# First weight block on ScalarE's queue in halves, input rows 1 and 2 issued behind row 0, row 1 cast in halves

## The chip, the cores and the metric

The kernel runs on one core of one Trainium2 chip. The metric is the device time of one execution in microseconds (us), as the median of several runs. The engines are TensorE (PE in the profile; its weight loads are PEld), VectorE (DVE), ScalarE (ACT), GpSimd (POOL) and SyncE (SP). Loads are issued by the queues of SP, ACT or POOL and are carried by 16 DMA engines.

## The reference

One decoder block with two token mixers and a SwiGLU. The input is 512 tokens of width 1024 in float32; the depth is one layer.

```python
h = rms_norm(x, norm_mix_pre[l])
proj = h @ w_in[l]
(g_q, g_k, g_v, g_r, g_a, n_q, ..., n_gate, merge_gla, merge_nsa) = jnp.split(proj, split_points, axis=-1)
o_gla = gla_mixer(g_q, g_k, g_v, g_r, g_a, ...)      # chunked gated linear attention, 4 heads
o_nsa = nsa_mixer(n_q, ..., n_gate, ...)             # compressed + selected + window attention, 8 heads
mixed = (jax.nn.sigmoid(merge_gla) * (o_gla @ w_proj_gla[l])
         + jax.nn.sigmoid(merge_nsa) * (o_nsa @ w_proj_nsa[l]))
x = x + rms_norm(mixed @ w_out[l], norm_mix_post[l])
h = rms_norm(x, norm_ffn_pre[l])
f = (jax.nn.silu(h @ w_ffn_gate[l]) * (h @ w_ffn_up[l])) @ w_ffn_down[l]
x = x + rms_norm(f, norm_ffn_post[l])
```

The change concerns how the first input and weights reach the first projection `h @ w_in`.

## The kernel before

**Arithmetic.** Each large product is made of three: an operand is split into a high part (a copy cast to float32r, mostly on ScalarE) and a low part (the remainder, a subtraction on VectorE), and TensorE adds high x high, high x low and low x high.

**Input.** The host passes x transposed, `xT`, as 8 blocks of 128 features by 512 tokens. Here such a block is called row k of the input. Each is loaded into `X[:, k]` on SP's queue (line 258); ScalarE writes its high part `hT` with the norm's gain `g_pre` as a scale (line 261), VectorE the low part `hTl` (line 262). The gain is part of `vecs`, loaded on ScalarE's queue (line 145). The rms factor is applied later, to the products. Before the loop stand `warm`, a small Exp on ScalarE (line 143, with the table load that it brings), and eight products `spin` on TensorE (line 148).

**Weights.** `Stream` loads and splits the weights in an order planned ahead: `ahead_to` takes a raw tile `wraw` (three buffers), calls `fetch` to issue its load on SP's queue, and issues the cast (line 79) and the subtraction (line 85). The first block, `("tok", 0, 0)`, holds 880 columns: 440 for row 0 and 440 for row 1. It alone stands in `halved`: it is loaded in two halves (line 55), the first half is cast on VectorE and the second on ScalarE (line 73), and both are subtracted on VectorE (line 74). In the loop over k, `ahead_to` is called at k = 0 for the first block and at k = 2 for the second, so SP's issues come in this order:

```
row 0, first half of block 0, second half of block 0, row 1, row 2, block 1, row 3, ..., row 7, block 2
```

**First products.** `tok_chunk` (lines 314 to 316) makes the first token-wise projection: for each of 4 blocks of 128 tokens and each row k, three products of 440 columns, into four PSUM banks (`ps_mm`, `ps_sc`). Four such chunks use the 8 rows. After it comes the same with 368 columns (into `ps_tp`, `ps_acc`), and then the paired projections at line 412, whose weight forms are prepared by ScalarE and VectorE at lines 224, 348, 351, 382 and 383, with raw weights loaded at line 344.

**Order.** The Tile framework takes the instructions in the order of the text as priorities and, when the program is built, fixes an order on each engine by what is ready; `issue_after` and `high_priority` in the text put single instructions behind or ahead. All waits are derived from the data.

Of the kernel before, what the change touches and what calls it, by code (L numbers as in the profile page):

```python
# [8 lines left out]
F32 = mybir.dt.float32  # L9
F32R = mybir.dt.float32r  # L10
U8 = mybir.dt.uint8
AF = mybir.ActivationFunctionType
# [24 lines left out]
class Stream:  # L37
# [7 lines left out]
    def plan(self, key, ap, cols):  # L45
        self.src.append((key, ap if isinstance(ap, list) else [ap], cols))

    def fetch(self, raw, aps):
        at = 0
        for ap in aps:  # L50
            n = ap.shape[-1]
            if len(ap.shape) == 3:
                self.nc.sync.dma_start(raw.rearrange("p (k n) -> p k n", k=2)[:, :, at:at + n], ap)
            else:
                self.nc.sync.dma_start(raw[:, at:at + n], ap)
            at += n

    def ahead_to(self, n):
        while self.made < min(n, len(self.src)):
            i = self.made  # L60
            key, aps, cols = self.src[i]
            raw = self.pool.tile([128, 1024], F32, tag="wraw", bufs=3, name="wraw")
            cut = self.halved.get(key, cols)
            parts = [slice(0, cut)] + ([slice(cut, cols)] if cut < cols else [])
            self.fetch(raw[:, :cols], [aps[0][:, p] for p in parts] if cut < cols else aps)
            if key in self.place:
                hi, lo = self.place[key]()
            else:
                hi = self.pool.tile([128, 1024], F32R, tag="whi", bufs=2, name="whi")
                lo = self.pool.tile([128, 1024], F32R, tag="wlo", bufs=2, name="wlo")  # L70
            if cut < cols:
                for p, copy in zip(parts, (self.nc.vector.tensor_copy, self.nc.scalar.copy)):
                    copy(hi[:, p], raw[:, p])
                    self.nc.vector.tensor_tensor(out=lo[:, p], in0=raw[:, p], in1=hi[:, p].bitcast(F32),
                                                 op=OP.subtract)
                self.done[i] = (hi, lo)
                self.made += 1
                continue
            self.cast = self.nc.scalar.copy(hi[:, :cols], raw[:, :cols])  # L79
            if key in self.on_dma:  # L80

                self.nc.scalar.activation(out=lo[:, :cols], in_=raw[:, :cols], func=AF.Copy, scale=-1.0)  # L82
                self.nc.gpsimd.dma_start(lo[:, :cols], raw[:, :cols], accum_op=OP.add)  # L83
            else:
                self.nc.vector.tensor_tensor(out=lo[:, :cols], in0=raw[:, :cols], in1=hi[:, :cols].bitcast(F32),  # L85
                                             op=OP.subtract)
            self.done[i] = (hi, lo)
            self.made += 1
# [24 lines left out]
def hybrid_block_kernel(ctx: ExitStack, tc: tile.TileContext, I, outT):  # L113
    nc = tc.nc
    act, dve, pool, pe = nc.scalar, nc.vector, nc.gpsimd, nc.tensor

    base = ctx.enter_context(tc.tile_pool(name="base", bufs=1, reuse_waits="tile"))
# [12 lines left out]
    mhalf = base.tile([128, 16], F32, name="mhalf")  # L130
# [8 lines left out]
        pool.dma_start(t, I[name])  # L139
        return t  # L140

    warm = base.tile([128, 1], F32, name="warm")
    act.activation(out=warm, in_=mhalf[:, 0:1], func=AF.Exp)
    vecs = base.tile([128, 4 * KD + HG + 2], F32, name="vecs")
    act.dma_start(vecs, I["vecs"])
    spin = bank("acc")
# [2 lines left out]
    g_pre, g_post = vecs[:, 0:8], vecs[:, 8:16]  # L149
    g_fpre, g_fpost = vecs[:, 16:24], vecs[:, 24:32]  # L150
    b_alpha, g_gla = vecs[:, 32:36], vecs[:, 36:38]
    hT = base.tile([128, KD, S], F32R, name="hT_hi")
# [27 lines left out]
    for key in with_gla + with_cmp + with_att + late:  # L180
        kind, n = key
# [74 lines left out]
    X = xin.tile([128, KD, S], F32, name="xt")  # L256
    for k in range(KD):
        nc.sync.dma_start(X[:, k], I["xT"][k])
        if k % 2 == 0:
            tk.ahead_to(min(k // 2 + 1, 2))  # L260
        last = act.activation(out=hT[:, k, :], in_=X[:, k], func=AF.Copy, scale=g_pre[:, k:k + 1])
        dve.scalar_tensor_tensor(out=hTl[:, k, :], in0=X[:, k], scalar=g_pre[:, k:k + 1],
                                 in1=hT[:, k, :].bitcast(F32), op0=OP.mult, op1=OP.subtract)
    p_mid = tc.tile_pool(name="mid", bufs=1, reuse_waits="tile")
# [1354 lines left out]
    for n in range(N0, KF):  # L1619
# [3 lines left out]
        last = unit(n, rest_of_forms if n == N0 else None)  # L1623
# [317 lines left out]
```

## Time and profile before

| | before |
|---|---|
| runs | 847.33 us median of 3 (847.05 to 847.94) |
| the profiled execution | 847.33 us |
| its span | 845.5 us |
| TensorE busy | 833.6 us (99%) |
| VectorE, ScalarE busy | 646.2 us (76%), 532.2 us (63%) |
| TensorE clock granted | 0.999 |
| loaded and stored | 119.96 MB, mean 142 GB/s |

The span goes from the first to the last instruction that the profile has; the rest of the execution's time lies around it. Times in the trace count from the span's start. In the order-of-time view a row has start, length, engine, line, operation and tiles; a bracket gives the engine's idle time ahead of it and what ended it. Rows of "SPq" or "ACTq" are issues of loads by those queues. In the view by stretches, a row gives for each engine the busy time and the number of instructions, then the granted clock, the mean busy share of the 16 DMA engines and GB/s.

### The profile page before, as it was taken

To read this page: it belongs to the slowest core of one execution; us is meant where nothing else is said; L and a number is where in the kernel's file an instruction comes from. 1 tells how busy PE (TensorE), PEld (TensorE's weight loads), DVE (VectorE), ACT (ScalarE), POOL (GpSimd) and SP (SyncE) were. 2 spreads that over 40 slices of the span, in tenths; PEclk is the share of its full clock that TensorE was granted. 3 is DMA by queue.
4 is the path that set the end of the run, shared out by engine and by line. 5 is a ranking of instruction groups with operands and counts; after the bars stand their busy time and mean duration, and the time that the engine had idled before them with its cause. 6 is when DMAs were issued, how large, how long until landed. Compare 5 with 4: busy or idle time off the path is not lost.

```text
span 845.5 us, 14860 instructions
## 1 busy us (share of the span) xinstructions
PE 833.6 (99%) x5640; PEld 763.4 (90%) x5640; DVE 646.2 (76%) x1209; ACT 532.2 (63%) x961; POOL 159.4 (19%) x194
## 2 busy tenths in 40 slices
PE   9999999999999999999999999999999999999997
PEld 8999999877888788788888998999999999889996
DVE  7877989845657888887685398998777779739885
ACT  7766686455635989887545587666555667435442
POOL 0223222322300010001001363021211110001433
PEclk9999999999999999999999999999999999999999
DMA  7688787211432445444238769488877762325222
GB/s 249 146 211 190 173 175 155 76 50 53 124 109 74 101 107 119 105 120 97 54 113 293 226 150 243 116 214 204 188 198 185 184 156 63 109 79 174 89 100 100
DMA packets 45017, 119.96 MB, mean 142 GB/s; under 512 B 5933, under 2 KB 11325, under 8 KB 44817
## 3 DMA queue, kind: packets, MB, share of 16 engines
q1 hardware_dynamic: 30576, 82.49, 30.6%
q0 software_dynamic: 13648, 35.98, 23.5%
q8 instruction: 44, 0.72, 0.3%
q10 hardware_dynamic: 720, 0.54, 0.2%
q14 instruction: 29, 0.23, 0.1%
HBM read 104.31 MB, written 4.19 MB: 128 GB/s over the span
## 4 chain that ended last, share of the span: by engine, by line
PE 85%; ACT 6%; DVE 5%; issue 2%; DMA 1%; POOL 1%; SPq 0%; DVEq 0%; ACTq 0%; POOLq 0%
PE ps_mm L1481 6%; PE ps_mm L207 6%; PE ps_mm L209 6%; PE ps_mm L208 6%; PE ps_sc L1481 6%; PE ps_tp L1481 6%; PE ps_acc L1481 5%; PE ps_sc L1773 4%; PE ps_mm L412 3%; PE ps_tp L412 3%; PE ps_sc L412 2%; PE ps_acc L1773 2%; PE ps_mm L1773 2%; PE ps_acc L412 2%; PE ps_tp L1082 2%
## 5 line engine op out<-in xcount | busy, mean ns | idle before, releaser
L79 ACT CAST whi<-wraw 128x1024 fp32r<-128x1024 f32 (+3 forms) x58 | 56.3, 971 | 52.9 <-issue 18.5
L207 PE MATMUL ps_mm<-hT_hi,whi 128*128 128x512 f32 x168 | 68.5, 408 | 0.0
L209 PE MATMUL ps_mm<-hT_hi,wlo 128*128 128x512 f32 x168 | 66.2, 394 | 0.0
L208 PE MATMUL ps_mm<-hT_lo,whi 128*128 128x512 f32 x168 | 66.2, 394 | 0.0
L85 DVE TENSOR_TENSOR wlo<-wraw,whi 128x1024 fp32r<-128x1024 f32 (+3 forms) x43 | 47.0, 1093 | 21.3 <-ACT whi L79 21.2
L83 POOL DMA_DIRECT2D wlo<-wraw x15 | 12.9, 862 | 157.1 <-ACT wlo L82 157.1
L1042 ACT ACTIVATE p<-p,mx 128x512 f32<-128x512 f32 (+1 forms) x64 | 35.9, 560 | 8.8 <-DVE mx L1040 8.2
L225 DVE TENSOR_TENSOR pl<-ps_tp,ph 128x512 fp32r<-128x512 f32 (+1 forms) x64 | 31.0, 489 | 13.2 <-ACT ph L224 12.6
L209 PEld LDWEIGHTS ps_mm<-hT_hi,wlo 128*128 128x128 f32 x168 | 31.5, 188 | 7.1 <-DVE wlo L85 0.3
L207 PEld LDWEIGHTS ps_mm<-hT_hi,whi 128*128 128x128 f32 x168 | 31.6, 188 | 6.0
L208 PEld LDWEIGHTS ps_mm<-hT_lo,whi 128*128 128x128 f32 x168 | 31.7, 189 | 5.0
L1040 DVE CUSTOM_DVE_ANT_0 p<-ps_sc,causal 128x512 f32<-128x512 f32 (+1 forms) x64 | 30.2, 485 | 6.2 <-PE ps_sc L1033 5.9
L1380 POOL DMA_DIRECT2D w_uu<-in_w_up x19 | 16.4, 865 | 89.3 <-ACT w_uu L1378 20.4
L224 ACT CAST ph<-ps_tp 128x512 fp32r<-128x512 f32 (+1 forms) x64 | 26.4, 415 | 4.1 <-PE ps_tp L1082 3.5
L1082 PE MATMUL ps_tp<-ident,p 128*128 128x128 f32 x160 | 27.7, 273 | 0.4 <-ACT pc L976 0.2
L1082 PEld LDWEIGHTS ps_tp<-ident,p 128*128 128x128 f32 x160 | 20.6, 140 | 8.1 <-ACT pc L976 0.7
L1396 ACT CAST w_d1h<-s 128x1024 fp32r<-128x1024 f32 x13 | 13.6, 1049 | 20.6 <-issue 12.7
L207 PE MATMUL ps_mm<-gla_hi,whi 128*128 128x512 f32 x64 | 26.2, 409 | 0.0
L209 PE MATMUL ps_mm<-gla_hi,wlo 128*128 128x512 f32 x64 | 25.2, 394 | 0.0
L208 PE MATMUL ps_mm<-gla_lo,whi 128*128 128x512 f32 x64 | 25.2, 393 | 0.0
L1396 ACT CAST w_hl<-s 128x1024 fp32r<-128x1024 f32 x12 | 12.6, 1047 | 16.6 <-issue 14.7
L1396 ACT CAST w_d0h<-s 128x1024 fp32r<-128x1024 f32 x13 | 13.6, 1047 | 13.8 <-issue 12.7
(1234 smaller groups left out, 3363.9 us busy)
## 6 DMA issues: line engine op xcount, KB each, us to landing
wraw<-in_w_t SPq DMA_DIRECT2D x29, 512.0 KB, 3.7
wraw<-in_w_gate SPq DMA_DIRECT2D x21, 512.0 KB, 5.7
rw<-in_w_up SPq DMA_DIRECT2D x19, 512.0 KB, 4.2
wlo<-wraw POOLq DMA_DIRECT2D x15, 512.0 KB, 4.5
wlo<-in_w_gate POOLq DMA_DIRECT2D x13, 512.0 KB, 7.1
urw<-in_w_t SPq DMA_DIRECT2D x11, 512.0 KB, 5.6
w_uu<-in_w_up POOLq DMA_DIRECT2D x19, 256.0 KB, 5.7
wraw<-in_w_proj SPq DMA_DIRECT2D x8, 512.0 KB, 3.5
```

What stands on the lines that cost most here:

```text
L79: self.cast = self.nc.scalar.copy(hi[:, :cols], raw[:, :cols])
L85: self.nc.vector.tensor_tensor(out=lo[:, :cols], in0=raw[:, :cols], in1=hi[:, :cols].bitcast(F32), op=OP.subtract)
L207: pe.matmul(ps[:, t], wh[:, c], xh(k)[:, t], start=(k == 0), stop=False)
L208: pe.matmul(ps[:, t], wh[:, c], xl(k)[:, t], start=False, stop=False)
L209: marks.append(pe.matmul(ps[:, t], wl[:, c], xh(k)[:, t], start=False, stop=(k == ktot - 1)))
L225: dve.tensor_tensor(out=lo, in0=src, in1=hi.bitcast(F32), op=OP.subtract)
L412: pe.matmul(o, w[:, c], x_of(b, q, low), start=(first and q == 0 and i == 0), stop=(q == 3 and i == 2), skip_group_check=True)
L1042: act.activation(out=o, in_=o, func=AF.Exp, scale=-1.0, bias=mx[:, i:i + 1], accum_out=z[:, i:i + 1])
L1082: pe.transpose(tp[:, i * 128:(i + 1) * 128], p[:, OFF[i] + k * 128:OFF[i] + (k + 1) * 128], ident)
L1396: act.copy(hi, t)
L1481: pe.matmul(o, w[:, c], x[q], start=(first and q == 0 and i == 0), stop=(q == 3 and i == 2), skip_group_check=True)
L1773: pe.matmul(o, w[:, c], x[q], start=(first and q == 0 and i == 0), stop=(q == KH - 1 and i == 2), skip_group_check=True)
```

## The change

The halves of block 0 are issued by ScalarE's queue instead of SP's; rows 1 and 2 thereby stand directly behind row 0 on SP's. `warm` moves from ahead of the vectors' load into the loop, behind block 0's loads. Row 1's high part is written by two instructions of 256 tokens each in place of one of 512. The rest is as before.

```diff
-    def fetch(self, raw, aps):
+    def fetch(self, raw, aps, queue=None):
         at = 0
+        queue = queue or self.nc.sync
         for ap in aps:
             n = ap.shape[-1]
             if len(ap.shape) == 3:
-                self.nc.sync.dma_start(raw.rearrange("p (k n) -> p k n", k=2)[:, :, at:at + n], ap)
+                queue.dma_start(raw.rearrange("p (k n) -> p k n", k=2)[:, :, at:at + n], ap)
             else:
-                self.nc.sync.dma_start(raw[:, at:at + n], ap)
+                queue.dma_start(raw[:, at:at + n], ap)
             at += n
...
-            self.fetch(raw[:, :cols], [aps[0][:, p] for p in parts] if cut < cols else aps)
+            if cut < cols:
+                self.fetch(raw[:, :cols], [aps[0][:, p] for p in parts], self.nc.scalar)
+            else:
+                self.fetch(raw[:, :cols], aps)
...
-    warm = base.tile([128, 1], F32, name="warm")
-    act.activation(out=warm, in_=mhalf[:, 0:1], func=AF.Exp)
     vecs = base.tile([128, 4 * KD + HG + 2], F32, name="vecs")
     act.dma_start(vecs, I["vecs"])
...
         nc.sync.dma_start(X[:, k], I["xT"][k])
         if k % 2 == 0:
             tk.ahead_to(min(k // 2 + 1, 2))
-        last = act.activation(out=hT[:, k, :], in_=X[:, k], func=AF.Copy, scale=g_pre[:, k:k + 1])
+        if k == 0:
+            warm = base.tile([128, 1], F32, name="warm")
+            act.activation(out=warm, in_=mhalf[:, 0:1], func=AF.Exp)
+        for t in (slice(0, 256), slice(256, 512)) if k == 1 else (slice(0, 512),):
+            last = act.activation(out=hT[:, k, t], in_=X[:, k, t], func=AF.Copy, scale=g_pre[:, k:k + 1])
         dve.scalar_tensor_tensor(out=hTl[:, k, :], in0=X[:, k], scalar=g_pre[:, k:k + 1],
                                  in1=hT[:, k, :].bitcast(F32), op0=OP.mult, op1=OP.subtract)
```

## The prediction

> **What bounds the kernel now.** I read first the page's busy shares and its chain, then the start in order of time, then the load rates by stretch, and last the chain between 20 and 110 us.
>
> ```profile
> span 845.5 us, 14860 instructions
> PE 833.6 (99%) x5640; PEld 763.4 (90%) x5640; DVE 646.2 (76%) x1209; ACT 532.2 (63%) x961; POOL 159.4 (19%) x194
> PE 85%; ACT 6%; DVE 5%; issue 2%; DMA 1%; POOL 1%; SPq 0%; DVEq 0%; ACTq 0%; POOLq 0%
> ```
>
> TensorE is busy 99% of the span and carries 85% of the chain. The edit touches the first microseconds alone, so what it can win is TensorE's idle time there, if later work keeps it. The start, in order of time (start, length, instruction; in brackets the idle time before and who ended it):
>
> ```profile
> 0.74 0.41 ACTq L145 DMA_DIRECT2D vecs<-in_vecs  x1
> 0.74 0.38 SPq L258 DMA_DIRECT2D xt<-in_xT  x1
> 0.92 3.63 PE L148 MATMUL ps_acc<-ones 128*128 128x128 f32 x16 [0.92 <-DVE eps L135]
> 1.18 0.89 SPq L55 DMA_DIRECT2D wraw<-in_w_tok  x2
> 1.18 1.28 ACT L143 ACT_TABLE_LOAD   x1 [1.18 <-PEq L1932]
> 2.11 0.91 SPq L258 DMA_DIRECT2D xt<-in_xT  x2
> 2.47 0.20 ACT L143 ACTIVATE warm<-mhalf 128x1 f32<-128x1 f32 x1
> 3.06 0.43 SPq L55 DMA_DIRECT2D wraw<-in_w_tok  x1
> 3.94 0.72 ACT L261 ACTIVATE hT_hi<-xt,vecs 128x512 fp32r<-128x512 f32 x1 [1.27 <-DMA vecs<-in_vecs]
> 4.29 0.39 DVE L73 CAST whi<-wraw 128x440 fp32r<-128x440 f32 x1 [3.33 <-DMA wraw<-in_w_tok]
> 4.82 0.64 PE L314 MATMUL ps_mm<-whi,hT_hi 128*128 128x440 f32 x2 [0.28 <-DVE whi L73]
> 5.98 0.56 ACT L73 CAST whi<-wraw 128x440 fp32r<-128x440 f32 x1 [1.31 <-DMA wraw<-in_w_tok]
> 6.57 0.62 DVE L74 TENSOR_TENSOR wlo<-wraw,whi 128x440 fp32r<-128x440 f32 x1 [0.59 <-ACT whi L73]
> 6.62 1.38 ACT L261 ACTIVATE hT_hi<-xt,vecs 128x512 fp32r<-128x512 f32 x2
> 6.70 0.37 PE L316 MATMUL ps_sc<-wlo,hT_hi 128*128 128x440 f32 x1
> 7.40 0.67 PE L314 MATMUL ps_mm<-whi,hT_hi 128*128 128x440 f32 x2 [0.33 <-ACT hT_hi L261]
> 7.91 0.36 PE L314 MATMUL ps_sc<-whi,hT_hi 128*128 128x440 f32 x1
> 8.42 0.93 ACT L79 CAST whi<-wraw 128x880 fp32r<-128x880 f32 x1 [0.42 <-DMA wraw<-in_w_tok]
> ```
>
> Row k of the input and half k of the first weight block belong together. TensorE starts on row 0 at 4.82, when both first casts are done (3.94 + 0.72 = 4.66; 4.29 + 0.39 = 4.68). Ten of the twelve products of row 0 start from 4.82 to 6.70, 0.20 us apart once the first has gone; the next could start near 6.90. It starts at 7.40, behind the cast of row 1 (6.62 to 7.34), and the one after near 7.71. So at 7.91, where twelve have started, some 0.6 us are lost (7.91 - 4.82 - 12 x 0.20 = 0.69, less about 0.1 that a first product takes longer). That is all that lies open here.
>
> **What the loads do.** Rates by stretch (the last three figures of a row are the granted clock, the DMA share and GB/s), and three rows of the load issues (KB each, us from issue to landing):
>
> ```profile
> 0.00:2.50 2.50, 1.58 (x7) 1.58 (x8) 0.15 (x4) 1.31 (x2) 0.69 (x6) 1.00 0.22 34
> 2.50:3.00 0.50, 0.50 (x4) 0.50 (x3) 0.00 (x0) 0.17 (x1) 0.00 (x0) 1.00 1.04 367
> 3.00:3.50 0.50, 0.50 (x4) 0.50 (x4) 0.00 (x0) 0.00 (x0) 0.00 (x0) 1.00 1.06 391
> 3.50:4.00 0.50, 0.50 (x4) 0.50 (x4) 0.00 (x0) 0.06 (x1) 0.00 (x0) 1.00 1.03 338
> 4.00:5.00 1.00, 0.72 (x5) 0.56 (x4) 0.69 (x2) 0.66 (x1) 0.00 (x0) 1.00 0.94 238
> 5.00:6.00 1.00, 1.00 (x6) 0.94 (x6) 0.98 (x2) 0.02 (x1) 0.00 (x0) 1.00 1.03 399
> ...
> xt<-in_xT SPq DMA_DIRECT2D x8, 256.0 KB, 5.6
> wraw<-in_w_tok SPq DMA_DIRECT2D x2, 220.0 KB, 3.7
> vecs<-in_vecs ACTq DMA_DIRECT2D x1, 19.0 KB, 3.2
> ```
>
> From 2.5 us on the DMA engines are full (share about 1). SP's issue of row 1 ends 0.42 us after it begins, yet the row is used only at 6.62, 4.5 us after its issue at 2.11: it stood in line for bandwidth, not for the issuing engine. With KB of 1024 bytes, rows 0 and 1, both halves and the vectors are 0.262 + 0.262 + 0.225 + 0.225 + 0.019 = 0.994 MB. The rates give 0.872 MB by 5.0 us, so the last of these bytes comes at 5.3, about 1.3 us before it is used. No order of issue makes 0.994 MB come sooner.
>
> **The edits, one by one.**
>
> SP: two issues leave its queue (1.18 to 2.11), so row 1 is issued at about 1.18, row 2 at 1.62, the second weight block at 2.13 instead of 3.06, and all later rows 0.93 earlier. POOL's queue is not passed: it issues nothing that early.
>
> ACT: the two halves go behind the vectors, at about 1.18 and 1.60 (0.41 each by the row at L145). Nothing blocks them, as their buffers are fresh. Behind them stands the table load: 2.03 to 3.31, then warm 0.20 to 3.52. Before, warm ended at 2.67. The cover is the wait for the vectors until 3.94 (0.74 + 3.2), with 0.4 left; so I cost it at nothing. Without that cover it would cost up to the 0.85 by which it moves.
>
> The trace has warm starting at 2.47, with the load over at 1.18 + 1.28 = 2.46. The Trainium skill (ScalarE: Activation LUTs, What ACT_TABLE_LOAD costs) gives a switch of set about 2.66 us, a drain included; by it the casts would begin near 4.9. This row shows no drain behind the load.
>
> Sharing: two queues now feed the same full engines. No row shows two large loads of different queues at once. The ends are that SP's queue goes first or that ScalarE's does; I take the middle, halves of the rate. From 2.7 (the first half block follows row 0 by 0.44, as its issue does) row 0 has 0.12 MB left of 0.281 with the vectors; at half of 380 GB/s that takes until 3.35, where alone it was done at 3.03. The wait for row 0's cast is put down to the vectors, so part of this slip is hidden; whole, it gives a cast from 4.26 to 4.98. The first half block has 0.10 MB left at 3.35 and is done at 3.89 instead of 3.62: its cast on DVE slips from 4.29 to 4.56 and ends at 4.95, and TensorE's start from 4.82 to about 5.09. Row 1 shares on, and is done at 5.1 instead of 5.3; the second half block at 5.4 instead of 4.4, because row 2 stands beside it for its last 0.065 MB. With 1.3 to 1.57 us to use (the latter is 5.98 - 4.41) row 1 is there at 6.4, and the second half block at 6.75 to 7.0. What is late next is therefore this half block: it had been there at 5.98 and now takes the place of row 1.
>
> The Trainium skill (DMA: Bandwidth & Descriptors, Issuing engines are not separate DMA queues) says that loads of several issuers run on the same 16 engines and interleave, and only issue time is saved. By it the sum is the one just made; the full share above agrees.
>
> The cast of row 1 in halves needs a duration that the start doesn't show:
>
> ```profile
> L1287 ACT ACTIVATE h2h<-slot,vecs x16: 491/506/512, 486.6 to 508.4; 128x256 fp32r<-128x256 f32 x16
> ```
>
> The same kind of operation on 256 columns takes 0.51 where 512 take 0.72. The first half is ready 0.2 us sooner; the second, begun about 0.42 behind the first, 0.2 later. Row 1's low part on DVE waits for both, so it slips 0.2 from its place; the products with the low part follow the high ones by more than that.
>
> Sum: the casts of the second half block end at 6.75 to 7.0 + 0.56 = 7.3 to 7.56, row 1's first half at about 6.9. Products of row 1 can start at 7.35 to 7.6. If the order on TensorE puts all twelve of row 0 ahead, these run from 5.09 to about 7.6 and nothing stands still: 0.3 gained against 7.91. If ten stand ahead, as now, the eleventh starts at 7.35 to 7.6 against 7.40: nothing to 0.2 lost. I take 0.1 gained. The ends: start unmoved and no wait gives 7.91 - 4.82 - 2.5 = 0.6 gained; both half blocks later by 0.5 (row 2 and the second block served ahead) gives 0.5 lost.
>
> Does later work keep it? From 7.91 the products follow each other 0.2 apart, and the chain goes from TensorE's use of a weight buffer into casts:
>
> ```profile
> 28.14 0.14 PE ps_tp L316
> 28.29 0.71 ACT whi L79
> 28.99 0.95 ACT s0h L348
> ...
> 33.11 0.93 DVE wlo L85
> ...
> 34.05 4.92 DMA wraw<-in_w_t
> ...
> 45.53 1.24 DVE s2l L383
> ...
> 46.81 5.26 PE ps_mm L412 x42
> ```
>
> These steps hang one on another, so a shift at 8 us arrives at 46.81 whole. The profiled execution took 847.33 us, which is the median of the runs; 845.5 is its span and 1.8 lies around it. 847.33 - 0.1 = 847.2.
>
> **The rivals.**
>
> A, the likeliest: the bandwidth is dealt out differently, nothing that can be told from no change comes of it (0.2% is 1.7 us, about what a measurement of this kernel can tell). 847.2, between 846.7 (0.6 gained) and 847.8 (0.5 lost).
>
> B, the change does what its words say: row 1 lands well ahead, the start doesn't slip, and the wait at 7.40 is gone. 0.6 gained, 846.7. For it: SP is 0.93 earlier. Against it: the full DMA share.
>
> C, slower: the order on each engine is made when the program is built and doesn't follow the text. The text has the cast of the second half block ahead of row 0's cast, while the rows at 3.94 and 5.98 show the opposite. Moved loads can thus change the order later. The place is the release of the buffer at 33.11: TensorE meets the end of this chain at 46.81 with no slack, as it waited there. If one form's cast and its subtraction came ahead of the cast at 28.29 or the subtraction at 33.11, it would cost 0.95 and 1.24 (the rows at 28.99 and 45.53): 2.2 in all, 849.5. It decides from one such pair on; a single cast stays within 0.2%.
>
> TensorE's own row at that place gives the wait ahead of it:
>
> ```profile
> 46.81 0.39 PE L412 MATMUL ps_mm<-t3h,s2l 128*128 128x256 f32 x1 [0.29 <-DVE s2l L383]
> ```
>
> D, faster by more than 0.2%: only if the order changes to the good in the same place or later. TensorE's two idle times here, 0.6 at the start and the 0.3 that the trace gives ahead of 46.81, don't reach 1.7 even together, so it would take a third place; with 2 us won in all, 845.3.
>
> E, the table load is no longer covered: casts begin 0.85 later, and TensorE with them. 848.0, if a wait that the trace of before doesn't show stands behind the load. The Trainium skill's page ScalarE: Activation LUTs, as told above, would have it so.
>
> **How the numbers follow.** A 0.58, B 0.15, E 0.05, C 0.13, D 0.09. A, B and E are within 0.2% of 847.33 (845.6 to 849.0), so same is 0.78, slower 0.13, faster 0.09. The range holds A, B and E with the spread of the runs shown (847.05 to 847.94, 0.3 below and 0.6 above the median): 846.4 to 848.6. It leaves out C and D, about 0.2.
>
> **What would show it.** Right: row 1 issued near 1.2 us; the DMA share still 1 from 2.5; the first product at 4.9 to 5.2, later than 4.82; the second half block's cast after 6.4 instead of 5.98; the thirteenth product at 7.6 to 8.1; the last steps of the chain as before, shifted by as much. Wrong: the first product before 4.8 and no wait ahead of row 1's (B); the table load's end past 3.9 (E); another order of casts between 25 and 46 us, or a wait of TensorE near 46 that grew by over 1 us (C) or went away along with others (D). What most easily makes me wrong is the order that the build makes, which no row of before can show.

## The result and the profile after

The changed kernel takes 852.51 us (851.59 to 853.3, 4 runs) against 847.36 (847.05 to 847.94, 4 runs): ratio 1.006, interval 1.0048 to 1.0072, so 5.15 us slower. The profiled execution took 852.11, its span 850.3, at a granted clock of 1.0. The line numbers of the changed kernel and of the experiments are shifted: line 314 became 320, 261 became 267, 73 became 77, 207 became 209. The page's head:

```profile
span 850.3 us, 14862 instructions
PE 837.8 (99%) x5640; PEld 765.2 (90%) x5640; DVE 644.7 (76%) x1209; ACT 532.5 (63%) x962; POOL 161.8 (19%) x194
```

TensorE has the same 5640 products, but is busy 4.2 us longer (833.6 before). The loss is thus partly time in which products run slower, not time in which they wait. The start of the changed kernel in order of time:

```profile
0.74 0.42 ACTq L147 DMA_DIRECT2D vecs<-in_vecs  x1
0.74 1.33 SPq L260 DMA_DIRECT2D xt<-in_xT  x3
1.18 0.93 ACTq L56 DMA_DIRECT2D wraw<-in_w_tok  x2
2.15 1.28 ACT L265 ACT_TABLE_LOAD   x1 [2.15 <-issue]
3.44 0.20 ACT L265 ACTIVATE warm<-mhalf 128x1 f32<-128x1 f32 x1
3.68 0.72 ACT L267 ACTIVATE hT_hi<-xt,vecs 128x512 fp32r<-128x512 f32 x1
5.78 0.39 DVE L77 CAST whi<-wraw 128x440 fp32r<-128x440 f32 x1 [4.82 <-DMA wraw<-in_w_tok]
6.31 1.07 PE L320 MATMUL ps_mm<-whi,hT_hi 128*128 128x440 f32 x2 [1.61 <-DVE whi L77]
7.18 0.94 PE L320 MATMUL ps_sc<-whi,hT_hi 128*128 128x440 f32 x2
7.92 0.57 PE L321 MATMUL ps_mm<-whi,hT_lo 128*128 128x440 f32 x1
8.04 0.56 ACT L77 CAST whi<-wraw 128x440 fp32r<-128x440 f32 x1 [3.65 <-DMA wraw<-in_w_tok]
8.28 0.57 PE L322 MATMUL ps_mm<-wlo,hT_hi 128*128 128x440 f32 x1
9.07 0.74 PE L320 MATMUL ps_mm<-whi,hT_hi 128*128 128x440 f32 x1 [0.22 <-ACT hT_hi L267]
10.12 0.36 PE L320 MATMUL ps_mm<-whi,hT_hi 128*128 128x440 f32 x1
```

Three things differ from before. Row 0's cast starts early (3.68, before 3.94), but its weights are not there: the start of the first half's cast goes from 4.29 to 5.78, that of the second half's from 5.98 to 8.04. TensorE starts at 6.31 instead of 4.82. And from 6.31 to about 9.9 a product takes 0.57 and the next follows 0.36 behind (7.92, 8.28); from 9.92 on it takes 0.36 and follows 0.20 behind, as in all of the start before.

The lag is found by setting the same-numbered products side by side. The 25th product of 440 columns starts at 10.30 before and 13.12 now, 2.8 later; TensorE's last pair of products starts 4.76 later. The rows of before:

```profile
10.30 0.36 PE L314 MATMUL ps_mm<-whi,hT_hi 128*128 128x440 f32 x1
...
840.84 0.70 PE L1821 MATMUL ps_acc<-slot,ident 128*128 128x256 f32 x2
```

and of the changed kernel:

```profile
13.12 0.36 PE L320 MATMUL ps_mm<-whi,hT_hi 128*128 128x440 f32 x1
...
845.60 0.70 PE L1827 MATMUL ps_acc<-slot,ident 128*128 128x256 f32 x2
```

Between these the lag is 2.76 at 28 us, 2.15 at 47 us, 2.1 at 165, 2.7 at 250, 2.9 at 440, 4.0 at 500, 4.2 at 720 and 5.3 at 760. So there are two losses: 2.8 us in the first 13 us, of which 0.6 is won back at 47 us, and some 2.6 more, nearly all of it in three stretches far from the edit (220 to 250, 440 to 500 and 725 to 760 us). The order of the instructions differs only at the start: up to about 50 us on TensorE (some 260 products), up to about 55 on VectorE and ScalarE. Behind that it is the same on every engine. The second loss is therefore not one of order. The groups of products by line show it; before (busy us and mean ns of one behind the first bar):

```profile
L207 PE MATMUL ps_mm<-hT_hi,whi 128*128 128x512 f32 x168 | 68.5, 408 | 0.0
L209 PE MATMUL ps_mm<-hT_hi,wlo 128*128 128x512 f32 x168 | 66.2, 394 | 0.0
```

and in the changed kernel:

```profile
L209 PE MATMUL ps_mm<-hT_hi,whi 128*128 128x512 f32 x168 | 69.1, 411 | 0.0
L211 PE MATMUL ps_mm<-hT_hi,wlo 128*128 128x512 f32 x168 | 66.5, 396 | 0.0
```

The same products, in the same order and at the same granted clock, take 2 to 3 ns more. The 192 products with these operands that go into `ps_acc` and `ps_tp` take 5 to 7 ns more (389 to 390 before, 395 to 396 now). Over all 696 of both kinds the durations in the trace add up to 275.7 us before and 278.0 now, 2.3 us more. What the edit changes for them is the place of their operand: tiles of `base` get their addresses in the order of the text. With `warm` allocated behind `vecs`, `hT_hi`, `hT_lo`, `rb_x` and `rs_x` instead of ahead of them, these five lie 32 bytes lower in each partition; `hT_hi` goes from byte 17376 to 17344.

### The profile page after: what moved, and what is told of

Its sections match the earlier page's. It is cut to its first block, busy times and chain, and to the rows that moved or that the text cites. A ratio compares the mean times of both kernels' runs of the same rounds, so it can differ in the third digit from the quotient of the medians.

```text
span 850.3 us, 14862 instructions
## 1 busy us (share of the span) xinstructions
PE 837.8 (99%) x5640; PEld 765.2 (90%) x5640; DVE 644.7 (76%) x1209; ACT 532.5 (63%) x962; POOL 161.8 (19%) x194
## 4 chain that ended last, share of the span: by engine, by line
PE 86%; ACT 5%; DVE 4%; issue 2%; DMA 1%; POOL 1%; ACTq 0%; DVEq 0%; POOLq 0%
PE ps_mm L1487 6%; PE ps_mm L209 6%; PE ps_mm L210 6%; PE ps_sc L1487 6%; PE ps_mm L211 6%; PE ps_tp L1487 6%; PE ps_sc L1779 4%; PE ps_acc L1487 4%; PE ps_mm L418 3%; PE ps_tp L418 3%; PE ps_sc L418 3%; PE ps_acc L1779 2%; PE ps_mm L1779 2%; PE ps_acc L418 2%; PE ps_tp L1088 2%
```

## The experiments

Two theories. Place: the later loss (some 2.6) comes from the 32 bytes, whatever the loads do. Start: the early loss (2 to 3) comes from ScalarE's queue, and place has no part in it. The rivals are that `warm` or the cast in halves costs the time.

### Place

**The place alone.** The kernel before, `warm` allocated last:

```diff
-    warm = base.tile([128, 1], F32, name="warm")
-    act.activation(out=warm, in_=mhalf[:, 0:1], func=AF.Exp)
     vecs = base.tile(...)
...
     rs_x = base.tile([128, NT], F32, name="rs_x")
+    warm = base.tile([128, 1], F32, name="warm"); act.activation(out=warm, in_=mhalf[:, 0:1], func=AF.Exp)
```

> The kernel before, with warm's tile given its slot behind rs_x instead of ahead of vecs, so that vecs, hT_hi, hT_lo, rb_x and rs_x lie 32 bytes lower per partition (hT_hi at 17344 instead of 17376), as in the changed kernel; the order on every engine stays. Theory place (the later 2 us of the loss come from where hT lies): first product at 4.8 us as before, the products of 512 columns with hT_hi some 2.5 ns longer in the mean, 849 to 850 us. Rival queue (the later loss follows from the moved loads) and rival drift (it is spread between executions): 847.0 to 847.8 us and no slower products.

Measured: 849.68 (849.54 to 849.86), ratio 1.0029 (1.0018 to 1.0041), on 847.23 for the kernel before: 2.45 us by place alone, with no edit of a load. Two stretches of the kernel before (us, then busy time and count of PE, PEld, DVE, ACT, POOL; granted clock, DMA share, GB/s):

```profile
440.00:497.00 57.00, 56.44 (x396) 52.18 (x395) 32.77 (x51) 35.36 (x64) 16.71 (x21) 1.00 0.69 222
725.00:762.00 37.00, 37.00 (x165) 30.61 (x165) 18.57 (x24) 13.27 (x20) 0.00 (x0) 1.00 0.31 100
```

and of this one:

```profile
440.00:497.00 57.00, 57.00 (x390) 52.34 (x389) 32.36 (x51) 33.92 (x61) 14.97 (x18) 1.00 0.70 222
725.00:762.00 37.00, 37.00 (x160) 29.82 (x159) 17.77 (x25) 11.56 (x17) 0.00 (x0) 1.00 0.36 107
```

In equal time TensorE gets 6 and 5 products fewer done, at the same granted clock, and in the first stretch with less idle time. These are the stretches in which the changed kernel's lag grows.

**The place undone.** The changed kernel, `warm`'s tile ahead of `vecs` again, its activation still in the loop:

```diff
+    warm = base.tile([128, 1], F32, name="warm")
     vecs = base.tile(...)
...
         if k == 0:
-            warm = base.tile([128, 1], F32, name="warm")
             act.activation(out=warm, in_=mhalf[:, 0:1], func=AF.Exp)
```

> The changed kernel with warm's tile back in its old slot ahead of vecs (its instruction stays in the loop), so hT_hi is at 17376 again; the order on every engine is that of the changed kernel. Theory place: the lag of 2.8 us at 10 us stays, it is about 2.1 us from 50 us to the end, 849.5 to 850.5 us. Rivals queue and drift: the lag grows by 2 us after 160 us as in the changed kernel, 852 to 853 us.

Measured: 851.12 (849.83 to 851.31), ratio 1.0042 (1.0029 to 1.0054). The later part came as the place theory has it: the products with `hT_hi` are back at 408 ns, and the lag, 3.57 at 50 us, is 3.78 at the end. The total is above the expected range, because the start of the profiled execution was worse: products at half rate until about 13.5 us, lag 4.3 at 15 us. The totals alone don't show the 2.45 of the place: undoing it takes the time only from 852.51 to 851.12.

```profile
L209 PE MATMUL ps_mm<-hT_hi,whi 128*128 128x512 f32 x168 | 68.5, 408 | 0.0
```

**Which tile.** The kernel before, with `warm`'s two lines behind the load of `vecs` (only `vecs` 32 lower), or between `hT` and `hTl` (`vecs` and `hT_hi` 32 lower).

> The kernel before with warm's tile between vecs and hT_hi: vecs lies 32 bytes lower, hT_hi (17376), hT_lo, rb_x and rs_x where they were. Theory place of hT: 847.0 to 847.8 us, no lag in the stages around 230, 470 and 740 us. Rival place of vecs: 849.3 to 850 us with the lags of r7_addr.

> The kernel before with warm's tile between hT_hi and hT_lo: vecs and hT_hi 32 bytes lower (hT_hi at 17344), hT_lo, rb_x and rs_x where they were. If the place of the high part alone makes it: 849.3 to 850 us. If the low part or rb_x makes it: 847.0 to 847.8. If both take part, between.

Measured: 847.19, ratio 0.9997 (0.9988 to 1.0006), and 850.11, ratio 1.0032 (1.002 to 1.0043). It is the place of `hT_hi`. With it alone lower, its products are slow again:

```profile
L209 PE MATMUL ps_mm<-hT_hi,whi 128*128 128x512 f32 x168 | 69.2, 412 | 0.0
```

**Which places.** More small tiles moved behind `rs_x` (64, 96 and 128 bytes lower), then `rs_x` allocated ahead of `hT` (32 higher), and `rb_x` ahead of `hT` (2048 higher, the length of one row of `hT`):

```diff
+    rb_x = base.tile([128, S], F32, name="rb_x")
     hT = base.tile([128, KD, S], F32R, name="hT_hi")
     hTl = base.tile([128, KD, S], F32R, name="hT_lo")
-    rb_x = base.tile([128, S], F32, name="rb_x")
```

> The kernel before with warm's and eps1's tiles behind rs_x, so that hT_hi is at 17312, 64 bytes lower than before and 32 lower than in r7_addr; the order is as before but for one fill on VectorE. Theory parity (whi and wlo are at 212960 and 221152, an odd multiple of 32, as hT at 17376 and 17312; at 17344 it is an even one, and that costs): 846.9 to 847.8 us. Rival lower (the lower the slower): 849.5 us or more.

> The kernel before with the tiles of eps4, eps1 and warm behind rs_x, hT_hi at 17280, 96 bytes lower. Theory distinct (the old place is a good one and any other costs): 849 to 850 us. Theory period (the cost repeats with 128 bytes; 32 and 64 lower were slow, 96 is untried): between 847 and 850, and only 128 lower must be as before.

> The kernel before with mhalf, eps1 and warm behind rs_x (eps4 moves too), hT_hi at 17248, 128 bytes lower. Theory period of 128 bytes: 846.9 to 847.8 us, no slower products in the stages around 230, 470 and 740 us. Theory distinct: 849 us or more.

> The kernel before with rs_x's tile ahead of hT_hi: hT_hi at 17408, 32 bytes higher, hT_lo and rb_x as much; the order on every engine is as before. Theory distinct (the old place is a good one): 849 us or more. Rival lower (only lower places are slow): 847.8 us or less, perhaps under the kernel before.

> The kernel before with rb_x's tile ahead of hT_hi: hT_hi at 19424, 2048 bytes (one row of it) higher, hT_lo as much; the order is as before. If only the place within 2048 bytes counts: 846.9 to 847.8 us and products of 408, 394 and 394 ns. If the exact place counts: 849 us or more.

Measured:

| `hT_hi` at byte | against before | us | ratio (interval) |
|---|---|---|---|
| 17248 | -128 | 850.11 | 1.0032 (1.002 to 1.0044) |
| 17280 | -96 | 851.37 | 1.005 (1.0037 to 1.0062) |
| 17312 | -64 | 849.23 | 1.0024 (1.0016 to 1.0033) |
| 17344 | -32 | 849.68 | 1.0029 (1.0018 to 1.0041) |
| 17408 | +32 | 849.46 | 1.0022 (1.0013 to 1.0031) |
| 19424 | +2048 | 847.28 | 1.0001 (0.9993 to 1.001) |

Neither guess about the place holds: that an even or odd count of 32 bytes decides (64 lower is slow too), or that the cost repeats every 128 bytes. Every shift by less than 2048 that was tried costs 2 to 4 us (of the 4.0 at -96 the profiled execution lost 0.8 by 10 us, with products at half rate at the start); the one by 2048 costs nothing, and its products have the old mean:

```profile
L209 PE MATMUL ps_mm<-hT_hi,whi 128*128 128x512 f32 x168 | 68.5, 407 | 0.0
```

Both good places are 992 past a multiple of 2048. What is good about 992, and against which other access it is so, stays open.

### The parts of the edit at the start

**The halves back on SP's queue**, all else as changed (place too):

```diff
-                self.fetch(raw[:, :cols], [aps[0][:, p] for p in parts], self.nc.scalar)
+                self.fetch(raw[:, :cols], [aps[0][:, p] for p in parts])
```

> The changed kernel with the first block's halves back on SP's queue; warm's move and row 1's cast in halves stay, hT at 17344. Theory sharing (the first half lands late since it stands behind the vectors on ScalarE's queue and beside rows 1 and 2): first product at 4.8 us, no products at half rate. With theory place 849 to 850 us, without it 846.9 to 847.6. Rival table (the moved table load and warm delay the start): first product after 5.3 us.

Measured: 849.92 (849.62 to 850.18), ratio 1.0032 (1.002 to 1.0045). The place alone gave 849.68 on the same chip. So, with the halves on SP's queue, `warm` in the loop and the cast in halves cost 0.2 together, within the spread; as causes by themselves these rivals fall. TensorE starts at 4.68, at full rate:

```profile
4.68 0.65 PE L320 MATMUL ps_mm<-whi,hT_hi 128*128 128x440 f32 x2
```

It waits 1.13 us ahead of row 1 at 7.86, as the second half was cast at 6.65 there; the lag at 10 us is 0.6 nevertheless.

**ScalarE's queue alone.** The kernel before, only the halves on ScalarE's queue; `warm` ahead, row 1 cast whole:

> The kernel before with the first block's halves on ScalarE's queue alone; warm stays ahead, row 1's cast whole, hT at 17376. Theory sharing: first half's cast after 5.5 us, first product at 6.0 to 6.5, products at half rate until about 10 us, lag 2.5 to 3.1 us there. With theory place 849.3 to 850.3 us, without it 852 to 853. Rival table: the start as before, 847.3 us.

Measured: 848.53 (847.95 to 849.56), ratio 1.0017 (1.0008 to 1.0026). Expected were half rate and 849.3 or more; both were missed. The first half is nearly as late as in the changed kernel (5.55 against 5.78), but after an idle time of the same length the products follow at full rate:

```profile
5.36 0.72 ACT L267 ACTIVATE hT_hi<-xt,vecs 128x512 fp32r<-128x512 f32 x1 [0.87 <-DMA xt<-in_xT]
5.55 0.39 DVE L77 CAST whi<-wraw 128x440 fp32r<-128x440 f32 x1 [0.28 <-DMA wraw<-in_w_tok]
6.09 0.44 PE L320 MATMUL ps_mm<-whi,hT_hi 128*128 128x440 f32 x1 [1.56 <-ACT hT_hi L267]
6.37 0.36 PE L321 MATMUL ps_mm<-whi,hT_lo 128*128 128x440 f32 x1
6.56 0.36 PE L320 MATMUL ps_mm<-whi,hT_hi 128*128 128x440 f32 x1
...
7.03 0.55 ACT L77 CAST whi<-wraw 128x440 fp32r<-128x440 f32 x1
```

Row 1 was cast at 5.36 here, ahead of the second half (7.03); in the changed kernel ScalarE's order has the second half first, and row 1 stands behind it although its data is there. The lag is 0.87 at 10 us and 1.1 at the end, and none of it comes from the later stretches.

### What the first half waits for

In the changed kernel the halves stand on ScalarE's queue behind the vectors, which are 128 packets of 152 bytes. Theories: the vectors ahead hold them up; or row 1, which now stands ahead on SP's queue, takes the bandwidth. The time to be explained differs between executions with the same order of loads: the first half is cast at 5.78 in the profile of the changed kernel, at 5.18 with the place undone, and at 4.90 with the place undone and 12 products `spin` (below).

**The vectors off ScalarE's queue**, in the kernel with the place undone: `nc.sync.dma_start(vecs, ...)`, ahead of row 0.

> r8_slot with the vectors issued by SP's queue ahead of row 0, so that ScalarE's queue carries the halves alone. Theory vectors: first half's cast on DVE at 4.2 to 4.7 us, first product 4.7 to 5.2 (row 0 may set it then, one issue later). Theory sharing: the cast at 5.1 us or later.

**Row 1 held back** in the same kernel, by two fills of its tile on POOL ahead of the load.

> r8_slot with row 1's load held on SP's queue by two fills of its tile on GpSimd (some 0.5 us each), so that rows 1 and 2 and block 1 are issued after the halves; block 1 comes ahead of row 2. Theory sharing (rows 1 and 2 take the half blocks' bandwidth): first half's cast on DVE at 4.4 to 4.8 us, first product at 4.8 to 5.2. Rival vectors (the halves stand behind the vectors' small packets on ScalarE's queue): the cast at 5.1 us or later, as in the changed kernel.

**The vectors between the halves**, with 12 products `spin`:

> r3_spin12 (halves on ScalarE's queue, hT at 17376, 12 spin products) with the vectors issued between the halves, so that the first half leads its queue. Theory vectors: first half's cast on DVE at 3.4 to 4.3 us; row 0's cast, which needs the vectors, at 3.9 to 4.6; first product behind the spin, at 5.5 us; the second half, behind the vectors, cast at 6.5 to 7.5. 848.3 to 849.4 us. It would be faster than 847.3 only if the second half came before 6 us.

Measured: 848.22 (847.13 to 851.23), ratio 1.0015 (1.0005 to 1.0026); 855.34 (854.59 to 856.84), 1.0098 (1.0084 to 1.0111); 849.43 (848.86 to 850.80), 1.0023 (1.0014 to 1.0032). Without the vectors ahead, and with its issue 0.45 earlier for that, the first half is cast at 3.46, though with them on SP's queue row 0 comes only at 4.86:

```profile
0.73 0.90 ACTq L56 DMA_DIRECT2D wraw<-in_w_tok  x2
3.46 0.39 DVE L77 CAST whi<-wraw 128x440 fp32r<-128x440 f32 x1 [2.50 <-DMA wraw<-in_w_tok]
4.86 0.72 ACT L267 ACTIVATE hT_hi<-xt,vecs 128x512 fp32r<-128x512 f32 x1 [1.70 <-DMA xt<-in_xT]
5.63 1.10 PE L320 MATMUL ps_mm<-whi,hT_hi 128*128 128x440 f32 x2 [0.92 <-ACT hT_hi L267]
```

Here SP's queue has the small packets: from 2.0 to 3.4 us it moves 0.17 MB in 172 packets, ScalarE's 0.26 MB in 163.

Holding row 1 can't tell the theories apart. The order made in the build put its load behind all others (issued at 7.40), so that TensorE waited for it; but row 2 and the second block took its place, and SP's queue was as full as before (0.35 MB from 2.0 to 3.4 us, against 0.34 with the place undone alone). The first half was cast at 5.08, hardly earlier than 5.18.

With the vectors between the halves, the first half is cast at 4.34, its issue again 0.44 earlier, but then row 0's cast waits for the vectors until 5.36. From 2.0 to 3.4 us ScalarE's queue moves 0.14 MB there and SP's 0.20. So both theories hold in part. The packets of the first half in the traces show it: before, they start between 2.85 and 3.62; in the changed kernel the vectors' packets run from 2.37 to 3.16, and those of the first half from 3.28 to 4.81. It begins 0.43 later, behind the vectors, and takes 1.53 instead of 0.77, beside the rows. None of the orders tried has both the first half and row 0 early.

### The rate of the products

**More `spin`** (12 instead of 8) in the kernel with the place undone, and **fewer** (4) in the kernel before. If the idle time ahead of the first product brings the half rate, 12 take it away and 4 bring it.

> The kernel r8_slot (the changed kernel, hT back at 17376) with 12 spin products instead of 8, so that TensorE has work until about 6.3 us; the order is the same but for a few of row 0's products. Theory clock (the idle 1 to 1.6 us behind the spin let TensorE stay at or fall to half rate, and how long depends on the execution): first product at 5.7 to 6.5 us, 0.20 us from product to product from then on, lag 1.0 to 2.0 us at 10 us instead of 2.8 to 4.3, 848.0 to 849.3 us. Rival loads (the half rate comes from the loads or from waits, not from TensorE's idle time): products 0.37 us apart until 10 us or later, 850.5 to 851.5 us.

> The kernel before with 4 spin products instead of 8: loads, casts and places unchanged, TensorE idle from some 2.8 us to the first product. Theory clock: the first products of 440 columns are 0.37 us apart instead of 0.20 for 3 us or more, lag 1 to 4 us at 15 us and kept to the end, 848.3 to 851 us. Rival (half rate comes from the loads or from late halves): 0.20 us apart and 847.3 us as before.

Measured: 849.40 (849.12 to 849.86), ratio 1.0025 (1.0015 to 1.0035), and 849.20 (847.17 to 849.99), ratio 1.0019 (1.0011 to 1.0028). With 12 the first product is near where it was (5.61, with the place undone 5.71), and the next ones follow at full rate:

```profile
5.61 0.64 PE L320 MATMUL ps_mm<-whi,hT_hi 128*128 128x440 f32 x2
6.08 0.36 PE L320 MATMUL ps_sc<-whi,hT_hi 128*128 128x440 f32 x1
...
8.34 0.46 PE L320 MATMUL ps_mm<-whi,hT_hi 128*128 128x440 f32 x1 [1.02 <-ACT hT_hi L267]
```

The lag at 10 us was to be 1 to 2 and is about 2.35: what the rate gave back, the wait for row 1 (1.02 at 8.34) partly took. Over the whole run 12 products win 1.7 us (851.12 to 849.40). With 4 in the kernel before, nothing else edited, the first products are as slow as in the changed kernel, and the median loses 1.8:

```profile
4.63 1.07 PE L320 MATMUL ps_mm<-whi,hT_hi 128*128 128x440 f32 x2 [1.64 <-DVE whi L77]
5.51 0.94 PE L320 MATMUL ps_sc<-whi,hT_hi 128*128 128x440 f32 x2
```

That profile is of its fastest execution (847.17), in which the rate came back at about 7.5; the others were 1 to 3 us longer. So the half rate comes without any edit of the loads when the warm-up is shorter, and goes with the loads as changed when it is longer.

**What the clock's record says.** The view by stretches prints a clock of 1.00 at the start of every run, but the record itself begins later: its first row in each trace is the moment from which the full clock is granted, and ahead of it there is no row. That moment is where the rate changes (us; ends of products are modelled, so one can start a little ahead of the end before it):

| run | `spin` ends | first product | full clock granted at | last product start at half rate |
|---|---|---|---|---|
| before | 4.54 | 4.82 | 4.25 | none |
| ScalarE's queue alone | 4.53 | 6.09 | 4.21 | none |
| place undone, 12 `spin` | 5.85 | 5.61 | 5.10 | none |
| changed kernel | 4.70 | 6.31 | 9.85 | 9.07 |
| place undone | 4.70 | 5.71 | 13.47 | 12.98 |
| vectors on SP's queue | 4.71 | 5.63 | 9.22 | 8.73 |
| before, 4 `spin` | 3.00 | 4.63 | 7.51 | 6.97 |

So the half rate is TensorE at less than the full clock. Where the full clock came before `spin` ended, an idle time of 1.56 behind it did no harm; where it had not come by then, the products ran at half rate until it did. Each kernel has one trace, so how often each case comes is not known.

From 848.53 (queue alone, full rate) by 849.40 (all of the start's edits, full rate) to 851.12 (the same at half rate) one can estimate the early loss of the kernel with the place undone: 1.3 for the late halves, 0.9 for the order of casts on ScalarE, 1.7 for the rate. These are from medians of different sets of runs, and the count of `spin` differs, so this split is not shown. Nor is its sum, 3.9, the early loss of the changed kernel: of the 5.15 there, 2.69 are left with the halves back on SP's queue, so that the queue is worth about 2.5. The profiles of the two kernels differ in how long the half rate lasted, until 13.5 and 9.9 us.

## Why the prediction was wrong

**The sharing step failed first.** It put the first half 0.44 behind row 0, "as its issue does", and from there at half of the rate: cast at 4.56, TensorE at 5.09. The issue was as said (1.18), the data not. The packets of the changed kernel by queue (packets, MB, share), for 2.0 to 3.4, 3.4 to 5.2 and 5.2 to 7.9 us; q10 is ScalarE's queue, q1 SP's:

```profile
q1 hardware_dynamic: 193, 0.36, 70.6%
q10 hardware_dynamic: 150, 0.03, 14.8%
...
q10 hardware_dynamic: 165, 0.26, 51.0%
q1 hardware_dynamic: 172, 0.32, 45.7%
...
q1 hardware_dynamic: 382, 0.88, 85.5%
q10 hardware_dynamic: 117, 0.18, 18.7%
```

Until 3.4 us ScalarE's queue moves 150 packets but only 0.03 MB: the vectors, in small packets, in turn with SP's large ones. SP's queue meanwhile moves 0.36 MB. Only then does the half of the rate set in that I took for the whole time (0.26 against 0.32 MB). The first half starts at 3.28 where the sum had 2.7, and its last packet at 4.81 where the sum had it done at 3.89; row 1 and most of row 2 are carried by 5.2; and the casts come at 5.78 and 8.04 instead of 4.56 and 6.75 to 7.0. In the other kernels with both halves behind the vectors on ScalarE's queue the first cast came at 4.90 to 5.55, also later than the sum. The full DMA share, on which I based that no order brings the bytes sooner, says nothing of whose bytes come first.

The Trainium skill (DMA: Bandwidth & Descriptors, Queues, rings and completion order) has each DMA engine go round the queues packet by packet. The 150 packets with 0.03 MB against 193 with 0.36 MB agree: by that rule a queue of 152-byte packets gets turns, not bytes.

**TensorE's rate was not a term at all.** I counted 0.20 us per product from the first one. After the later start it was 0.36 until 9.9. The terms for the products of row 1 (7.35 to 7.6) and the thirteenth product (7.6 to 8.1) fell with it: row 1 starts at 9.07. The view by stretches hides this; it prints a granted clock of 1.00 there (third figure from the end), although the record's first row, full clock, is at 9.85:

```profile
6.30:9.00 2.70, 2.54 (x6) 1.80 (x6) 1.55 (x3) 0.95 (x3) 0.00 (x0) 1.00 1.04 397
```

The kernel with row 1 held has such a stretch inside its record, which begins there at 9.16 (three stretches, and two rows in order of time):

```profile
9.20:12.50 3.30, 0.67 (x4) 0.28 (x2) 3.24 (x6) 3.30 (x7) 0.00 (x0) 1.00 1.05 402
12.60:19.30 6.70, 5.89 (x15) 4.90 (x16) 3.34 (x7) 2.74 (x6) 0.00 (x0) 0.50 0.33 116
19.40:22.00 2.60, 2.60 (x14) 2.44 (x14) 2.60 (x5) 2.47 (x6) 0.00 (x0) 1.00 0.19 35
...
16.14 0.57 PE L322 MATMUL ps_mm<-wlo,hT_hi 128*128 128x440 f32 x1
16.51 0.57 PE L321 MATMUL ps_sc<-whi,hT_lo 128*128 128x440 f32 x1
```

TensorE was idle for 3.52 us ahead of 13.39, and the clock is 0.50 from 12.57 to 19.40. At this clock a product of 440 columns takes 0.57 and the next follows 0.37 behind, as at the start of the changed kernel: there too TensorE ran at half of its clock. The Trainium skill (TensorE: Matmul & The Clock Gate, Part 1: The HAM clock gate) gives a window of about 3.4 us that runs by itself, half of the clock after an idle one and the full clock after a busy one. The record agrees: its rows here are 3.41 and 6.83 us long, and the clock fell 2.7 us into the wait, at the end of a window in which TensorE was busy for 0.7.

Counted back from 9.85 in steps of 3.41, the changed kernel has a window from 3.02 to 6.44, in which TensorE waited from 4.70 to 6.31, and an almost busy one from 6.44 to 9.85, after which the full clock came. With ScalarE's queue alone the window that ended at 4.21 lay almost whole within `spin` (0.92 to 4.53), and the wait came after it. So the gap of about 1.6 counts in one kernel and not in the other by where the window falls. How much idle time a window may hold stays open: 0.53 did no harm in the kernel with 4 `spin` (from 4.10 to 4.63), while one with a wait of 0.52 (from 6.64 to 10.06, the place undone) didn't bring the full clock. No run moved the window by itself.

**The place was not considered.** The diff's move of `warm` was costed as work on ScalarE only. As an allocation it moves `hT_hi`, and that alone costs 2.45 us, beside 5.15 in all; it is by itself enough to end outside of the range given.

**"A shift at 8 us arrives at 46.81 whole"** was wrong by 0.6, to the good: of 2.76 at 28 us, 2.15 are left at 47. The wait of 0.29 ahead of 46.81 is gone, and the order up to there is another. Behind that point the shift does stay: with the place undone the lag is 3.57 at 50 us and 3.59 at 600.

**What held.** The table load cost nothing: load from 2.15 to 3.43, `warm` at 3.44, the cast of row 0 at 3.68; before 3.94. So E falls: `warm` starts 0.01 behind the load's end. The cast in halves costs nothing that can be told where the halves are on SP's queue. The second half block did take the place of row 1 as what comes late. C's mechanism, another order with a loss near 33 and 46 us, did not occur: the order differs, but the lag shrinks there. C's time of 849.5 was the nearest of the rivals, for another reason. A and B gave the start 0.1 to 0.6 of gain; it lost 2.8 by 13 us.

## What to carry to other kernels

Two queues on full DMA engines shared by packets here, so that a load behind one of many small packets began late, and then had half of the rate: look at bytes per queue in short windows, and at who stands ahead on the queue. Where TensorE waits in the start, price the wait by the rate of the products behind it as well, and take that rate from the distance of equal products: a printed clock of 1.00 says nothing where the record has not begun. And a moved allocation is an edit of its own: compare addresses and the mean time of products far from the edit before the cause is sought in it.

## What the runs showed that was not expected

The place of the moving operand: 32 bytes make products of 512 columns 2 to 3 ns longer (408 to 411, 394 to 396) in some stretches, 2.45 us in all; every place tried costs 2 to 4 us but for two that are 2048 bytes apart. And products that follow each other at 0.36 instead of 0.20 for up to 8 us, because the full clock, which the kernel before has from 4.25 us, was granted only at 7.5 to 13.5 us. No version tried beat the kernel before; the best were as fast (847.19 and 847.28).
